# Channel mixing by Strassen's seven products, in two phases

## The chip, the cores and the metric

The kernel runs on one core of one Trainium2 chip. Its engines are TensorE (PE in the profile; PEld are its weight loads), VectorE (DVE), ScalarE (ACT), GpSimd (POOL) and SyncE (SP, which only issues DMAs here). Each has its own queue and takes instructions in order; they wait for each other by semaphores. The metric is the device time of one execution in microseconds (us), the median of several runs.

## The reference

One layer of an encoder trunk on x of 1024 tokens by 1024 channels, float32: a token-mixing part (a gated delta rule beside a spatial gate, joined and projected by w_out, then a layer norm), and a channel-mixing part with a hidden width of 2816, which is all that the change touches:

```python
x = layer_norm(DEEPNORM_ALPHA * x + h @ w_out[l], ln1_g[l], ln1_b[l])
up = causal_depthwise_conv(x @ w_up[l], conv_ffn[l])          # w_up [1024, 5632], 3 taps
a_ff, b_ff = jnp.split(up, 2, axis=-1)
x = layer_norm(DEEPNORM_ALPHA * x + (jax.nn.silu(a_ff) * b_ff) @ w_down[l], ln2_g[l], ln2_b[l])
```

## The kernel before

A wide product keeps float32's accuracy by splitting each operand into a rounded part (hi, a cast on ScalarE) and the remainder (lo, a subtraction on VectorE that reads the operand and hi, both in SBUF), and adding hi·hi, hi·lo and lo·hi. That is `split` (L87 to 89). Every product of 128 x 128 weights with 512 columns is three matmuls.

The channel mixing (L873 on) goes through 22 blocks f of 128 hidden channels. `ffn_up(f)` loads and splits two weight blocks (`load_w`, L349: the a half and the b half), and makes two products of 1024 columns (`proj_half`, L363 to 369), 96 matmuls. The result stays in PSUM; the convolution reads it there, its first tap on ScalarE (L390), two on VectorE (L392). Then silu on ScalarE (L892), the multiplication by b on VectorE (L894), a split of the result into two SBUF slots, and a load and split of a row block of w_down (L903). `ffn_down` multiplies a group of two f (the last group has four) with its w_down rows and adds the result to y in SBUF on VectorE (L925, L927), 48 matmuls for each f. Group g - 1's down product stands behind the first up product of group g, so TensorE always has one while the other's operands are made. No activation of the channel mixing leaves SBUF. In the last group, each row block's layer norm follows its last product (L929 to 958).

The order of the work is set by a scheduler from the program's order and priorities; the W_out product ahead (L835) and its layer norm (`wout_end`) lead into the channel mixing.

Of the kernel before, what the change touches and what calls it, by code (L numbers as in the profile page):

```python
# [996 lines left out]
```

## Time and profile before

| | |
|---|---|
| device time, median of 3 runs | 1558.77 us (1558.72 to 1560.59) |
| span of the profiled execution | 1559.6 us |
| TensorE busy | 1512.3 us, 97% |
| VectorE, ScalarE, GpSimd busy | 54%, 26%, 16% |
| chain that ended last: TensorE's share | 83% |
| HBM read and written | 75.63 MB and 4.19 MB |

The profile is of one execution; its span is the time from the first to the last instruction. A window row gives the busy time of each engine in a stretch, a timeline row one instruction (or several alike) with its start and length, a group row the count, the total and the mean of all instructions of one line and shape, with the idle time of the engine ahead of them.

### The profile page before, as it was taken

What the parts mean: (1) busy time and instruction counts of PE and PEld (TensorE: products, weight loads), DVE (VectorE), ACT (ScalarE), POOL (GpSimd) and SP (SyncE); (2) the same over time, 40 slices, a digit from 0 to 9 for tenths busy, and PEclk for the clock granted to TensorE, in tenths of its full rate; (3) what the DMA queues carried; (4) which work ended last, traced back from release to release, by engine and by line L of the source; (5) the groups of instructions that cost most, each with busy time, mean ns of one, the idle gap of its engine ahead of it and who ended that gap; (6) DMA issues with size and microseconds to landing.
All of it is one profiled execution on the core that took longest, in us unless ns stands there. A gap on an engine that the chain in (4) does not pass through costs nothing.

```text
span 1559.6 us, 17452 instructions
## 1 busy us (share of the span) xinstructions
PE 1512.3 (97%) x7155; PEld 1239.2 (79%) x7155; DVE 841.5 (54%) x1357; ACT 410.7 (26%) x526; POOL 250.2 (16%) x322
## 2 busy tenths in 40 slices
PE   8999899989899999999999999999999999999997
PEld 8977777767778888887888888888888888888885
DVE  5848577785974112335664535455454454635457
ACT  3343333433432111223013211313122131221321
POOL 2344353543531000000210000000000000000007
PEclk9999999999999999999999999999999999999998
DMA  7011101110101111225001211212111020111102
GB/s 233 18 38 41 28 20 36 28 28 28 28 14 41 41 54 55 81 68 201 16 14 60 62 41 41 64 31 68 40 41 55 28 81 28 54 41 41 54 27 108
DMA packets 100798, 80.94 MB, mean 52 GB/s; under 512 B 4155, under 2 KB 90863, under 8 KB 100719
## 3 DMA queue, kind: packets, MB, share of 16 engines
q1 hardware_dynamic: 98991, 73.54, 15.6%
q10 hardware_dynamic: 1728, 6.29, 1.2%
q8 instruction: 56, 0.92, 0.2%
q14 instruction: 23, 0.19, 0.0%
HBM read 75.63 MB, written 4.19 MB: 51 GB/s over the span
## 4 chain that ended last, share of the span: by engine, by line
PE 83%; DVE 10%; DMA 2%; POOL 2%; issue 1%; ACT 1%; SPq 0%; DVEq 0%; POOLq 0%
PE mm L367 49%; PE sm L920 15%; PE mm L437 6%; PE mm L835 4%; PE mm L215 2%; DVE u L582 2%; DVE u L583 1%; DVE y L392 1%; PE sm L613 1%; PE sm L161 1%; PE sm L618 1%; DMA y<-in_x_dram 1%; DVE zz L526 1%; DVE xx L585 1%; DVE dd L524 1%
## 5 line engine op out<-in xcount | busy, mean ns | idle before, releaser
L367 PE MATMUL mm<-xh,wh 128*128 128x512 f32 x2560 | 653.2, 399 | 0.0
L367 PEld LDWEIGHTS mm<-xh,wh 128*128 128x128 f32 x2560 | 477.8, 189 | 101.1 <-issue 0.2
L367 PE MATMUL mm<-xh,wl 128*128 128x512 f32 x1280 | 344.4, 404 | 0.0
L367 PEld LDWEIGHTS mm<-xh,wl 128*128 128x128 f32 x1280 | 240.7, 190 | 54.3
L89 DVE TENSOR_TENSOR wl<-wr,wh 128x1024 fp32r<-128x1024 f32 x63 | 77.2, 1225 | 330.7 <-PE mm L367 285.7
L88 ACT CAST wh<-wr 128x1024 fp32r<-128x1024 f32 x63 | 66.1, 1050 | 486.1 <-PE mm L367 455.6
L221 POOL TENSOR_SCALAR rstd<-mv 128x1 f32<-128x1 f32 x24 | 21.0, 874 | 1043.0 <-DVE mv L817 1019.3
L927 DVE TENSOR_TENSOR y<-y,sm 128x512 f32<-128x512 f32 x144 | 97.2, 684 | 59.4 <-PE sm L920 59.4
L392 DVE SCALAR_TENSOR_TENSOR y<-mm,cf,y 128x1023 f32<-128x1023 f32 x88 | 112.6, 1280 | 16.1 <-ACT y L390 14.9
L920 PE MATMUL sm<-ob,dd 128*128 128x512 f32 x288 | 82.1, 394 | 0.0
L358 POOL TENSOR_TENSOR wl<-wr,wh 128x1024 fp32r<-128x1024 f32 x25 | 60.2, 2408 | 76.2 <-ACT wh L357 23.4
L920 PE MATMUL sm<-ob,kv 128*128 128x512 f32 x240 | 69.1, 395 | 0.0
L920 PE MATMUL sm<-ob,xx 128*128 128x512 f32 x240 | 68.7, 394 | 0.0
L920 PEld LDWEIGHTS sm<-ob,dd 128*128 128x128 f32 x288 | 54.0, 188 | 13.1 <-DVE dd L89 0.2
L390 ACT ACTIVATE y<-mm,cf 128x1024 f32<-128x1024 f32 x44 | 49.2, 1119 | 45.8 <-PE mm L367 45.8
L89 DVE TENSOR_TENSOR ob<-wr,ob 128x1024 fp32r<-128x1024 f32 x26 | 31.8, 1225 | 53.6 <-ACT ob L88 53.6
L920 PE MATMUL sm<-ob,gm 128*128 128x512 f32 x192 | 60.3, 395 | 0.0
L392 DVE SCALAR_TENSOR_TENSOR y<-mm,cq,y 128x1023 f32<-128x1023 f32 (+2 forms) x36 | 45.9, 1276 | 20.5 <-ACT y L390 20.2
L920 PEld LDWEIGHTS sm<-ob,xx 128*128 128x128 f32 x240 | 45.0, 188 | 10.9
L920 PEld LDWEIGHTS sm<-ob,kv 128*128 128x128 f32 x240 | 45.0, 188 | 10.8
L835 PE MATMUL mm<-ob,xh 128*128 128x512 f32 x192 | 47.9, 397 | 0.9 <-DVE y L842 0.9
L835 PEld LDWEIGHTS mm<-ob,xh 128*128 128x128 f32 x192 | 35.8, 188 | 9.6 <-DVE y L842 1.3
(303 smaller groups left out, 1902.9 us busy)
## 6 DMA issues: line engine op xcount, KB each, us to landing
wr<-in_w_up_dram SPq DMA_DIRECT2D x44, 512.0 KB, 3.7
wr<-in_w_in_dram SPq DMA_DIRECT2D x36, 512.0 KB, 3.9
wr<-in_w_down_dram SPq DMA_DIRECT2D x22, 512.0 KB, 3.5
y<-in_x_dram SPq DMA_DIRECT2D x8, 512.0 KB, 6.9
wr<-in_w_out_dram SPq DMA_DIRECT2D x8, 512.0 KB, 3.6
y<-in_x_dram ACTq DMA_DIRECT2D x8, 512.0 KB, 5.7
out_dram<-y SPq DMA_DIRECT2D x16, 256.0 KB, 2.0
ob<-in_w_in_dram SPq DMA_DIRECT2D x8, 256.0 KB, 5.4
```

The costliest lines, as they stand in the source:

```text
L88: nc.scalar.copy(hi, src)
L89: eng.tensor_tensor(out=lo, in0=src, in1=hi.bitcast(F32), op=ALU.subtract)
L215: nc.tensor.matmul(pp[:, 512 * i:512 * i + 260], st, mv[:, 260 * i:260 * i + 260], start=(k, a, b) == (0, 0, 0), stop=(k, a, b) == (KT - 1 ...
L358: nc.gpsimd.tensor_tensor(out=lo, in0=raw, in1=hi.bitcast(F32), op=ALU.subtract)
L367: nc.tensor.matmul(pp[:, half * 512:(half + 1) * 512], w[a][:, k, wcol:wcol + P], act[b][half][:, k], start=n == 0, stop=n == 3 * nk - 1)
L390: nc.scalar.activation(dst, pp, AF.Copy, scale=taps[n - 1])
L392: nc.vector.scalar_tensor_tensor(out=dst[:, s:], in0=pp[:, :S - s], scalar=taps[n - 1 - s], in1=dst[:, s:], op0=ALU.mult, op1=ALU.add)
L437: nc.tensor.matmul(pp[:, half * 512:(half + 1) * 512], w[a][:, k, wcol:wcol + P], o[k][b][:, half], start=n == 0, stop=n == 11)
L582: nc.vector.tensor_tensor(out=tmp[:, :, :i + 1], in0=LB[:, :, :i + 1, i], in1=x16[:, :, :i + 1], op=ALU.mult)
L835: nc.tensor.matmul(pp[:, nh * 512:(nh + 1) * 512], hT[a][half][:, k, off:off + P], wo[k][b][:, nh * 512:(nh + 1) * 512], start=k == 0 and ...
L920: nc.tensor.matmul(pd, f[a][:, m * P:(m + 1) * P], wd[b][:, nh * 512:(nh + 1) * 512], start=n == 0, stop=n == 3 * n_k - 1)
L927: nc.vector.tensor_tensor(out=ys, in0=ys, in1=pd, op=ALU.add)
```

## The change

Both products of the channel mixing go by one level of Strassen's algorithm (in Winograd's form): operands are cut into 2 x 2 blocks, and seven products of sums and differences of blocks take the place of eight.

In the up phase a product's left side is a weight block pair: a11 and a12 are the two halves (512 input channels each) of the a block of f, a21 and a22 those of the b block. Four sums s1 to s4 are formed on GpSimd (`sums`), and seven operands are split (`left_op`). The right sides B1 to B7 are blocks of x1 (the layer norm's output, transposed) and their differences, built once (`x1_first`, `x1_second`). Seven products of 12 matmuls go into PSUM banks X, Z and Y, some of them on top of what the bank holds, after ScalarE has copied it out. In the order of the program the products' left sides are a11, s1, s2, s4, s3, a12, a22: they are called the first to the seventh product. The convolution now reads SBUF. The result of f stays in SBUF until its pair is done; then four sums of the pair are formed on GpSimd, and seven blocks go to HBM (fd0 to fd6). The residual y goes there too (yd).

When all 22 f are done the SBUF places change hands: w_down (`DQ`) and y are loaded, and seven products follow, each over 11 pairs j, with the activations loaded from HBM block by block (`load_f`), split, and multiplied; a product's four banks are added to y at its end. Places of SBUF are reused as soon as what stood there has been read (`reuse_waits="tile"`).

```diff
+    def x1_first(m):
+        cols = slice(m * P, m * P + P)
+        raw = tl("y8", [2, 4, P])
+        for g, pt in enumerate(x1_blocks(m)):
+            half_split(B[(1, 2)[g]], cols, pt)
+            nc.scalar.copy(raw[:, g], pt)
+        first_half.append(raw)
+    def x1_second(m):
+        cols = slice((m - 4) * P, (m - 4) * P + P)
+        raw = first_half[m - 4]
+        p12, p22 = x1_blocks(m)
+        b12t4 = tl("wl", [2, 4, P])
+        t12 = tl("y8", [2, 4, P])
+        t3 = tl("y8", [4, P])
+        b12, t4 = b12t4[:, 0], b12t4[:, 1]
+        t1, t2 = t12[:, 0], t12[:, 1]
+        nc.scalar.copy(b12, p12)
+        nc.vector.tensor_tensor(out=t1, in0=p12, in1=raw[:, 0], op=ALU.subtract)
+        half_split(B[3], cols, p22)
+        nc.vector.tensor_tensor(out=t3, in0=p22, in1=b12, op=ALU.subtract)
+        nc.vector.tensor_tensor(out=t2, in0=p22, in1=t1, op=ALU.subtract)
+        nc.gpsimd.tensor_tensor(out=t4, in0=raw[:, 1], in1=t2, op=ALU.subtract)
+        half_split(B[5], cols, t1)
+        half_split(B[6], cols, t2)
+        half_split(B[7], cols, t3, nc.gpsimd)
+        half_split(B[4], cols, t4, nc.gpsimd)
...
+            B[1], B[2] = new_b(big, "xh", 4), new_b(big, "xh", 4)
             for i in range(4):
-                to_x1(i)
+                x1_first(i)
+    phase["sb"].close()
+    right = enter("right", side="right")
+    B[3], B[5] = new_b(big, "xh", 4), new_b(big, "xh", 4)
+    for i in (6, 7, 4):
+        B[i] = new_b(right, "xh2", 3)
     for m in range(4, NT):
-        to_x1(m)
+        x1_second(m)
...
+    def left_op(src):
+        op = right.tile([P, 2, 512], F32R, tag="op", name=name("op"), bufs=7)
+        split(op[:, 0], op[:, 1], src)
+        return op
+    def block_product(pp, a, b, first=False):
+        n = 0
+        for i, j in TERMS:
+            for k in range(4):
+                nc.tensor.matmul(pp, a[:, i, k * P:(k + 1) * P], b[:, j, k], start=first and n == 0, stop=n == 11,
+                                 skip_group_check=not first)
+                n += 1
+    def sums(s12, s34, a11, a12, a21, a22):
+        s1, s2, s3, s4 = s12[:, 0], s12[:, 1], s34[:, 0], s34[:, 1]
+        for o, a, b, op in ((s1, a21, a22, ALU.add), (s2, s1, a11, ALU.subtract), (s3, a11, a21, ALU.subtract),
+                            (s4, a12, s2, ALU.subtract)):
+            nc.gpsimd.tensor_tensor(out=o, in0=a, in1=b, op=op)
+        return s1, s2, s3, s4
+    def conv3(src, dst, f):
+        nc.scalar.activation(dst, src, AF.Copy, scale=cf[:, 2, f:f + 1])
+        for s in (1, 2):
+            nc.vector.scalar_tensor_tensor(out=dst[:, s:], in0=src[:, :S - s], scalar=cf[:, 2 - s, f:f + 1],
+                                           in1=dst[:, s:], op0=ALU.mult, op1=ALU.add)
+    H0, H1 = slice(0, 512), slice(512, 1024)
     def ffn_up(f):
+        ws = []
+        for c in (f, NF + f):
+            w = left.tile([P, 1024], F32, tag="wq", name=name("wq"), bufs=4)
+            nc.sync.dma_start(v3(w, KT), upsrc[:, :, c * P:(c + 1) * P])
+            ws.append(w)
+        a11, a12, a21, a22 = ws[0][:, H0], ws[0][:, H1], ws[1][:, H0], ws[1][:, H1]
+        s1, s2, s3, s4 = sums(yy([2, 512]), yy([2, 512]), a11, a12, a21, a22)
+        x, z, yb = bank("X", 3), bank("Z", 3), bank("Y", 2)
+        part, mid = yy([2, 512]), yy([512])
+        ca, cb = yy([S]), yy([S])
+        ta, tb = yy([S]), yy([S])
+        block_product(x, left_op(a11), B[1], True)
+        nc.scalar.copy(part[:, 0], x)
+        block_product(z, left_op(s1), B[5], True)
+        nc.scalar.copy(mid, z)
+        block_product(x, left_op(s2), B[6])
+        nc.scalar.copy(part[:, 1], x)
+        block_product(z, left_op(s4), B[3])
+        nc.vector.tensor_tensor(out=ca[:, H1], in0=z, in1=part[:, 1], op=ALU.add)
+        block_product(x, left_op(s3), B[7])
+        nc.vector.tensor_tensor(out=cb[:, H1], in0=x, in1=mid, op=ALU.add)
+        block_product(yb, left_op(a12), B[2], True)
+        nc.vector.tensor_tensor(out=ca[:, H0], in0=yb, in1=part[:, 0], op=ALU.add)
+        conv3(ca, ta, f)
+        nc.scalar.activation(ta, ta, AF.Silu)
+        block_product(x, left_op(a22), B[4])
+        nc.scalar.copy(cb[:, H0], x)
+        conv3(cb, tb, NF + f)
+        nc.vector.tensor_tensor(out=ta, in0=ta, in1=tb, op=ALU.mult)
+        return ta
+    for j in range(NF // 2):
+        f0 = ffn_up(2 * j)
+        nc.sync.dma_start(fd[0][j], f0[:, H0])
+        f1 = ffn_up(2 * j + 1)
+        s = sums(yy([2, 512]), yy([2, 512]), f0[:, H0], f1[:, H0], f0[:, H1], f1[:, H1])
+        for i, src in ((1, f1[:, H0]), (3, f1[:, H1]), (4, s[0]), (5, s[1]), (6, s[2]), (2, s[3])):
+            nc.sync.dma_start(fd[i][j], src)
+    for what in ("left", "ups", "right", "big"):
+        phase[what].close()
...
+    DQ = {}
+    for t in ("b11", "b12", "b22", "b21", "tt"):
+        DQ[t] = dn.tile([P, NJ, 512], F32, tag=t, name=t)
+    for t, two, hs in (("b11", 0, H0), ("b12", 0, H1), ("b22", 1, H1), ("b21", 1, H0)):
+        for c0, c1 in ((0, 2), (2, 4), (4, 7), (7, NJ)):
+            nc.sync.dma_start(DQ[t][:, c0:c1], dnsrc[two][:, c0:c1, hs])
+    y = []
+    for m in range(NT):
+        yt = dn.tile([P, D], F32, tag="y", name=name("y"), bufs=8)
+        nc.scalar.dma_start(yt, yd[m])
+        y.append(yt)
+    lt = dn.tile([P, 2, 1024], F32, tag="lt", name="lt")
+    nc.scalar.dma_start(lt[:, 0], ln2_g[0].partition_broadcast(P))
+    nc.scalar.dma_start(lt[:, 1], ln2_b[0].partition_broadcast(P))
...
+    def load_f(i, j):
+        t = dn.tile([P, 512], F32, tag="fq", name=name("fq"), bufs=6)
+        nc.sync.dma_start(t, fd[i][j])
+        return t
...
+    def down_product(banks, i, right_of, first=False):
+        for j in range(NJ):
+            a = split4(op4(), load_f(i, j))
+            b = split4(op4(), right_of(j))
+            for m in range(4):
+                for n, (p, q) in enumerate(TERMS):
+                    nc.tensor.matmul(banks[m], a[:, p, m * P:(m + 1) * P], b[:, q], start=first and j == 0 and n == 0,
+                                     stop=j == NJ - 1 and n == 2, skip_group_check=not first)
...
+    def t_sum(a, b, dst):
+        def make(j):
+            nc.gpsimd.tensor_tensor(out=DQ[dst][:, j], in0=DQ[a][:, j], in1=DQ[b][:, j], op=ALU.subtract)
+            return DQ[dst][:, j]
+        return make
...
+    X, Z = four("DX"), four("DZ")
+    down_product(X, 0, lambda j: DQ["b11"][:, j], True)
+    to_y(X, 0, H0)
+    down_product(Z, 4, t_sum("b12", "b11", "tt"), True)
+    to_y(Z, 1, H1)
+    down_product(X, 5, t_sum("b22", "tt", "tt"))
+    to_y(X, 0, H1)
+    down_product(Z, 2, lambda j: DQ["b22"][:, j])
+    to_y(Z, 0, H1)
+    down_product(X, 6, t_sum("b22", "b12", "b12"))
+    to_y(X, 1, H1)
+    Y = four("DZ")
+    for j in range(NJ):
+        t_sum("b21", "tt", "tt")(j)
+    down_product(Y, 1, lambda j: DQ["b21"][:, j], True)
+    to_y(Y, 0, H0)
+    for m in range(4):
+        st6 = dn.tile([P, 12], F32, tag="stl", name=name("stl"), bufs=4)
+        for i in range(2):
+            ln_half(y[m], st6, i)
+        finish(m, st6)
...
+        hi, lo, hw = (r[:, j] for r in res)
+        if j % 2 == 0:
+            pair = op4()
+        lw = pair[:, j % 2]
+        split(hi, lo, load_f(3, j))
+        split(hw, lw, DQ["tt"][:, j])
+        last.append(((hi, lo), (hw, lw)))
+    st = {m: dn.tile([P, 12], F32, tag="stl", name=name("stl"), bufs=4) for m in range(4, NT)}
+    for m in range(4, NT):
+        ln_half(y[m], st[m], 1)
+    for m in range(4):
+        for j in range(NJ):
+            for n, (p, q) in enumerate(TERMS):
+                nc.tensor.matmul(X[m], last[j][0][p][:, m * P:(m + 1) * P], last[j][1][q], start=False,
+                                 stop=j == NJ - 1 and n == 2, skip_group_check=True)
+        one_to_y(X[m], 4 + m, H0)
+        ln_half(y[4 + m], st[4 + m], 0)
+        finish(4 + m, st[4 + m])
```

The first place is GpSimd's queue. Before, there is nothing on it between the last rows of the first layer norm and the last layer norm at the kernel's end (mv and rstd are their statistics):

```order
L222 TENSOR_TENSOR rstd_872_6150<-rstd_872_6150,nhalf_107 128x1
L221 TENSOR_SCALAR rstd_876_6211<-mv2_875_6209 128x1
L222 TENSOR_TENSOR rstd_876_6211<-rstd_876_6211,nhalf_107 128x1
L221 TENSOR_SCALAR rstd_1366_10325<-mv2_1365_10323 128x1
L222 TENSOR_TENSOR rstd_1366_10325<-rstd_1366_10325,nhalf_107 128x1
L952 TENSOR_TENSOR mv2_1365_10323<-mv2_1365_10323,rstd_1366_10325 128x1
```

Now, at the pair of f = 2 and 3 and the next even f = 4 (yy_959 and yy_979 are the results of f = 2 and 3, yy_988 and yy_989 the pair's sums; wq_990 and wq_991 are the weights of f = 4, yy_992 and yy_993 their sums s1 to s4, wq_1010 and wq_1011 those of f = 5):

```order
L975 TENSOR_TENSOR yy_988_6955<-yy_959_6693,yy_979_6833 128x512
L975 TENSOR_TENSOR yy_989_6956<-yy_959_6693 128x512
L975 TENSOR_TENSOR yy_988_6955<-yy_988_6955,yy_959_6693 128x512
L975 TENSOR_TENSOR yy_992_6971<-wq_991_6969 128x512
L975 TENSOR_TENSOR yy_989_6956<-yy_979_6833,yy_988_6955 128x512
L975 TENSOR_TENSOR yy_992_6971<-yy_992_6971,wq_990_6967 128x512
L975 TENSOR_TENSOR yy_993_6972<-wq_990_6967,wq_991_6969 128x512
L975 TENSOR_TENSOR yy_993_6972<-wq_990_6967,yy_992_6971 128x512
L975 TENSOR_TENSOR yy_1012_7111<-wq_1011_7109 128x512
L975 TENSOR_TENSOR yy_1013_7112<-wq_1010_7107,wq_1011_7109 128x512
```

The weight sums of f = 4 stand behind three of the pair's sums, which need the finished yy_979.

The second place is ScalarE's queue. Before, while TensorE is at one f (y8_1048 and y8_1049 are the two halves of an f's convolution, wh and ob casts of weights, xx of an activation):

```order
L88 CAST wh_1056_7700<-wr_1055_7699 128x1024
L390 ACTIVATE y8_1048_7679<-mm_1046_7581,cf_101_893 128x1024
L892 ACTIVATE y8_1048_7679<-y8_1048_7679 128x1024
L88 CAST ob_1068_7824<-wr_1067_7823 128x1024
L88 CAST wh_1059_7706<-wr_1058_7705 128x1024
L390 ACTIVATE y8_1049_7680<-mm_1047_7582,cf_101_893 128x1024
L88 CAST xx_1050_7689<-y8_1048_7679 128x1024
```

Now, from the silu of f = 3 on (op_1004 to op_1009 are the operands of f = 4 from its second product on, op_1023 the first of f = 5; Z_995 and X_994 are banks of f = 4):

```order
L1011 ACTIVATE yy_979_6833<-yy_979_6833 128x1024
L111 CAST op_1004_7002<-yy_992_6971 128x512
L999 COPY yy_997_6980<-X_994_6977 128x512
L111 CAST op_1005_7018<-yy_992_6971 128x512
L111 CAST op_1006_7034<-yy_993_6972 128x512
L111 CAST op_1007_7050<-yy_993_6972 128x512
L111 CAST op_1008_7066<-wq_990_6967 128x512
L111 CAST op_1009_7086<-wq_991_6969 128x512
L111 CAST op_1023_7126<-wq_1010_7107 128x512
L1001 COPY yy_998_6981<-Z_995_6978 128x512
L1003 COPY yy_997_6980<-X_994_6977 128x512
```

The copy of bank Z, which holds the second product of f = 4, stands behind the casts of all of that f's operands and of the next f's first.

The third place is SP's queue where the phases meet. Before, the weights of up and down products come in turn:

```order
L355 DMA wr_1086_7957<-in_w_up_dram 128x8x128
L355 DMA wr_1089_7963<-in_w_up_dram 128x8x128
L903 DMA wr_1098_8081<-in_w_down_dram 128x1024
L355 DMA wr_1101_8087<-in_w_up_dram 128x8x128
L355 DMA wr_1104_8093<-in_w_up_dram 128x8x128
```

Now, from the last pair's blocks on (yy_9452 is the result of f = 21 and yy_9574, yy_9575 are the last pair's sums; b_9596 to b_9599 are the four quarters of w_down, fq an activation block of the first down product):

```order
L1024 DMA fd_5687<-yy_9574 128x512
L1024 DMA fd_5688<-yy_9574 128x512
L1024 DMA fd_5689<-yy_9575 128x512
L1024 DMA fd_5685<-yy_9575 128x512
L1039 DMA b_9596<-in_w_down_dram 128x2x512 x2
L1039 DMA b_9596<-in_w_down_dram 128x3x512
L1039 DMA b_9596<-in_w_down_dram 128x4x512
```

and, at the end of these loads:

```order
L1039 DMA b_9598<-in_w_down_dram 128x4x512
L1039 DMA b_9599<-in_w_down_dram 128x2x512 x2
L1039 DMA b_9599<-in_w_down_dram 128x3x512
L1039 DMA b_9599<-in_w_down_dram 128x4x512
L1051 DMA fq_9645<-fd_5683 128x512
L1051 DMA fq_9665<-fd_5683 128x512
```

The first activation block stands behind all sixteen loads of w_down, and these behind the last pair's stores.

## Rows read from the trace of the kernel before

**Rows 1.** The page: the span, part 1 (engines), the chain that ended last by engine.

```profile
span 1559.6 us, 17452 instructions
PE 1512.3 (97%) x7155; PEld 1239.2 (79%) x7155; DVE 841.5 (54%) x1357; ACT 410.7 (26%) x526; POOL 250.2 (16%) x322
PE 83%; DVE 10%; DMA 2%; POOL 2%; issue 1%; ACT 1%; SPq 0%; DVEq 0%; POOLq 0%
```

**Rows 2.** Windows: us, busy (x records) by engine, TensorE clock, DMA share, GB/s.

```profile
core 0: us, PE busy (x) PEld busy (x) DVE busy (x) ACT busy (x) POOL busy (x), PEclk, DMA share, GB/s
811.50:1548.40 736.90, 736.90 (x3201) 597.83 (x3199) 370.81 (x398) 173.96 (x167) 27.97 (x42) 1.00 0.16 49
900.00:1000.00 100.00, 100.00 (x434) 81.20 (x433) 45.93 (x47) 22.16 (x21) 0.00 (x0) 1.00 0.16 48
```

**Rows 3.** Timeline of TensorE where the channel mixing begins: start, duration, line.

```profile
810.75 0.85 PE L835 MATMUL mm<-xx,xh 128*128 128x512 f32 x3
811.44 1.91 PE L161 MATMUL sm<-ident,y 128*128 128x128 f32 x16
```

**Rows 4.** Groups by line and shape: engine, tiles, count; busy us, mean ns; idle before.

```profile
L88 ACT CAST xh<-y 128x512 fp32r<-128x512 f32 x16 | 8.8, 617 | 15.4 <-DVE y L794 9.5 <-PE mm L367 5.9
L89 DVE TENSOR_TENSOR xh<-y,xh 128x512 fp32r<-128x512 f32 x16 | 10.0, 685 | 5.3 <-PE mm L367 4.0 <-ACT xh L88 1.4
L88 ACT CAST xh<-sm 128x512 fp32r<-128x512 f32 x32 | 17.4, 592 | 68.2 <-PE sm L161 67.7
L390 ACT ACTIVATE y<-mm,cf 128x1024 f32<-128x1024 f32 x44 | 49.2, 1119 | 45.8 <-PE mm L367 45.8
L392 DVE SCALAR_TENSOR_TENSOR y<-mm,cf,y 128x1023 f32<-128x1023 f32 x44 | 56.3, 1280 | 14.9 <-ACT y L390 14.9
L894 DVE TENSOR_TENSOR y<-y,y 128x1024 f32<-128x1024 f32 x22 | 26.9, 1222 | 0.5
L933 POOL TENSOR_TENSOR y<-y,xh 128x512 f32<-128x512 f32 x14 | 17.8, 1291 | 1.2 <-DVE y L930 1.2
L927 DVE TENSOR_TENSOR y<-y,sm 128x512 f32<-128x512 f32 x144 | 97.2, 684 | 59.4 <-PE sm L920 59.4
```

**Rows 5.** Timeline of VectorE and GpSimd working beside each other, from 185.8 us.

```profile
185.83 1.05 POOL L481 TENSOR_TENSOR gm<-triM,gt 128x512 fp32r<-128x512 f32 x1 [1.81 <-PE sm L486]
185.92 2.04 DVE L424 TENSOR_TENSOR y<-y,ob 128x1024 f32<-128x1024 f32 x1
190.09 1.26 POOL L490 TENSOR_TENSOR dd<-dd,triS 128x512 f32<-128x512 f32 x1
190.15 1.74 DVE L685 TENSOR_TENSOR kv<-kv,rstd 128x512 f32<-128x512 f32 x1 [2.19 <-POOL rstd L222]
191.42 1.60 POOL L491 TENSOR_TENSOR dd<-dd,triM 128x512 f32<-128x512 f32 x1
```

**Rows 6.** Windows where TensorE restarts after idling (columns as in rows 2).

```profile
332.50:335.00 2.50, 0.49 (x2) 0.53 (x3) 1.82 (x4) 0.00 (x0) 1.58 (x2) 0.58 0.00 0
335.00:337.50 2.50, 2.50 (x9) 1.92 (x9) 0.57 (x2) 1.16 (x2) 0.68 (x1) 0.50 0.00 0
337.50:340.00 2.50, 2.50 (x14) 2.40 (x13) 1.94 (x11) 0.12 (x2) 0.00 (x0) 0.56 0.00 0
340.00:342.50 2.50, 2.50 (x15) 2.06 (x14) 1.82 (x2) 1.85 (x3) 1.49 (x1) 1.00 0.00 0
```

**Rows 7.** The same view of the first input loads, the densest DMA of the span.

```profile
12.00:15.00 3.00, 3.00 (x27) 3.00 (x26) 2.06 (x3) 0.74 (x2) 0.00 (x0) 1.00 1.03 412
```

**Rows 8.** The page, part 6: DMA issues, KB each, us from issue to landing.

```profile
wr<-in_w_up_dram SPq DMA_DIRECT2D x44, 512.0 KB, 3.7
```

**Rows 9.** Timeline of the span's end, from TensorE's last matmuls.

```profile
1547.59 0.86 PE L920 MATMUL sm<-ob,dd 128*128 128x512 f32 x3
1548.33 2.23 DVE L930 TENSOR_TENSOR y<-y,xh 128x1024 f32<-128x1024 f32 x1 [1.22 <-ACT y L954]
1550.48 0.67 DVE L927 TENSOR_TENSOR y<-y,sm 128x512 f32<-128x512 f32 x1
```

More of the change, by code (lines that the diff above doesn't have):

```diff
@@ L46, in trunk, with enter @@
     nc = tc.nc
-    sb = ctx.enter_context(tc.tile_pool(name="sb", bufs=1))
-    ps = ctx.enter_context(tc.tile_pool(name="ps", bufs=1, space=bass.MemoryType.PSUM))
+    keep = ctx.enter_context(tc.tile_pool(name="keep", bufs=1))
+    dr = ctx.enter_context(tc.tile_pool(name="dr", bufs=1, space=bass.MemoryType.DRAM))
+    phase = {}
+    def enter(what, **kw):
+        s = ExitStack()
+        phase[what] = s
+        return s.enter_context(tc.tile_pool(name=what, bufs=1, reuse_waits="tile", **kw))
+    big = enter("big")
+    sb = enter("sb", side="right")
+    act = enter("act")
+    ps = enter("ps", space=bass.MemoryType.PSUM)
+    KEEP = {"rstd", "mv2", "st6", "cf"}
+    POOL_OF = {"xh": big, "y8": act, "wr": act, "wh": act, "wl": act}
     count = [0]
@@ L800, in trunk @@
         load_wo((SLOTS[2 * k], SLOTS[2 * k + 1]))
-    lnp = [tl("y8", [D]) for _ in range(2)]
+    lnp = [tl("wh", [D]) for _ in range(2)]
     nc.scalar.dma_start(lnp[0], ln1_g[0].partition_broadcast(P))
@@ new lines, in trunk, with yy, bank @@
+    for m in range(4, NT):
+        x1_second(m)
+    phase["act"].close()
+    phase["ps"].close()
+    left = enter("left")
+    ps = enter("ups", space=bass.MemoryType.PSUM)
+    upsrc = w_up[0].rearrange("(k p) c -> p k c", p=P)
+    def yy(shape, dt=F32):
+        return left.tile([P] + shape, dt, tag="yy", name=name("yy"), bufs=11)
+    def bank(tag, bufs):
+        return ps.tile([P, 512], F32, tag=tag, name=name(tag), bufs=bufs)
+    def left_op(src):
+        op = right.tile([P, 2, 512], F32R, tag="op", name=name("op"), bufs=7)
+        split(op[:, 0], op[:, 1], src)
+        return op
@@ new lines, in trunk @@
+    ps = ctx.enter_context(tc.tile_pool(name="dps", bufs=1, space=bass.MemoryType.PSUM, reuse_waits="tile"))
+    NJ = NF // 2
+    dnsrc = w_down[0].rearrange("(j two p) c -> two p j c", two=2, p=P)
+    outv = out[0].rearrange("(t p) d -> t p d", p=P)
+    DQ = {}
[4 more added lines that the diff above has]
+            nc.sync.dma_start(DQ[t][:, c0:c1], dnsrc[two][:, c0:c1, hs])
@@ new lines, in four, with to_y, one_to_y @@
+    def four(tag):
+        return [ps.tile([P, 512], F32, tag=tag, name=name(tag), bufs=4) for _ in range(4)]
+    seen = set()
+    def to_y(banks, row, hs):
+        for m in range(4):
+            one_to_y(banks[m], 4 * row + m, hs)
+    def one_to_y(bank_, m, hs):
+        ys = y[m][:, hs]
+        if (m, hs.start) in seen:
+            nc.vector.tensor_tensor(out=ys, in0=ys, in1=bank_, op=ALU.add)
+        else:
+            seen.add((m, hs.start))
+            nc.vector.scalar_tensor_tensor(out=ys, in0=ys, scalar=ALPHA, in1=bank_, op0=ALU.mult, op1=ALU.add)
@@ new lines, in trunk @@
+    to_y(Y, 0, H0)
+    for m in range(4):
+        st6 = dn.tile([P, 12], F32, tag="stl", name=name("stl"), bufs=4)
+        for i in range(2):
+            ln_half(y[m], st6, i)
+        finish(m, st6)
+    last = []
+    res = [dn.tile([P, NJ, 512], F32R, tag=t, name=f"{t}r") for t in ("b11", "b12", "b22")]
+    for j in range(NJ):
[6 more added lines that the diff above has]
+        last.append(((hi, lo), (hw, lw)))
```

141 lines of the change are left out of this document (43 added, 98 removed).

## Prediction

> **What bounds the kernel now.** I read the page first: TensorE is busy for 97% of the 1559.6 us, and the chain that ended last runs through it for 83% [rows 1]. The windows say where: from the end of the W_out product to the last matmul of the kernel TensorE never idles, 736.9 of 736.9 us at full clock, and in a clean stretch it does 434 matmuls of 512 columns per 100 us, so 0.2304 us each [rows 2]. VectorE is half busy there, ScalarE a fifth, GpSimd not at all. The timeline puts the beginning of the stretch at 811.5 us [rows 3] and its end at 1548.4, with 11.2 us of last layer norm behind it [rows 9]. So matmuls taken away here come off the time in full, unless TensorE begins to wait. The rest of the argument is about waits, for which I take the durations of the operand work [rows 4], of VectorE beside GpSimd [rows 5], of the clock after idling [rows 6] and of dense DMA [rows 7, 8].
>
> **What goes.** Before: 22 x 96 matmuls up and 22 x 48 down, 3168. After: 7 products of 12 for each f, 22 x 84 = 1848, and 7 x 11 x 12 = 924 down, 2772. 396 x 0.2304 = 91.2 us go. 3168 x 0.2304 = 729.9 of the 736.9 us; the other 7.0 (transposes, mostly) stay. TensorE's own work after is 2772 x 0.2304 + 7.0 = 645.7 us. All up to 811.5 keeps its order.
>
> **What comes: the stall on each even f.** GpSimd now forms four weight sums for each f, and four sums of the finished activations for each pair; its queue has the pair's sums ahead of the next even f's weight sums (the first place shown with the change). The pair's sums wait for the product silu(a)·b of the odd f, which needs that f's seventh product. Call T the end of that product. ScalarE copies it (0.59), makes the first tap (1.12), VectorE two taps (2 x 1.28) and the multiplication (1.22): T + 5.5 [rows 4]. GpSimd's 512-column sum took 1.29, 1.26 and 1.05 in three places [rows 4, 5]; I take 1.25. Three of the pair's four sums: T + 9.3; the first weight sum of the even f: T + 10.5; its cast 0.62: T + 11.2. Meanwhile TensorE has only the first product of that f (12 x 0.2304 = 2.77, its operand is a raw block). So it idles from T + 2.8 to T + 11.2, 8.4 us.
>
> Then the fourth product. Its operand, the last of GpSimd's next four sums, would be ready at 15.5, and with two of VectorE's remainders (0.69 each) taking turns with them at T + 17. But the fourth product adds to bank Z, which still holds the second until ScalarE has copied it, and that copy stands on ScalarE behind the casts of s4, s3, a12, a22 and of the next f's a11 (the second place): 17 + 5 x 0.62 + 0.59 = T + 20.7. The last four products take 11.1: T + 31.8, where 7 x 2.77 = 19.4 would do. That is 12.4 us lost for each of f = 2, 4, ... 20: 10 x 12.45 = 125 us. The lower end is the first wait alone, 8.4 x 10 = 84; the upper end has 2 us more per stall (below), 145.
>
> The odd f have no such wait: their weight sums stand right behind and need only weights, which land 3.7 us after issue [rows 8], loaded an f ahead. Per f VectorE has 7 remainders x 0.685, 4 taps x 1.28, 1.22 and 3 additions from PSUM x 0.684, 13.2 us; 11.1 of them read two SBUF operands. GpSimd has 6 sums x 1.25 = 7.5. Each fits in 19.4. They do not run beside each other, though: a two-operand VectorE instruction of 1.22 took 2.04 when GpSimd was 0.1 us ahead of it, one of 0.69 took 1.74, and GpSimd's next took 1.60 [rows 5]. 11.1 + 7.5 = 18.6 of 19.4 still fits, with no room to spare. **The Trainium skill** (GPSIMD Engine Reference, Specifications) says that GpSimd shares its SBUF interfaces with VectorE and contends with VectorE instructions that have two SBUF inputs; this trace agrees (2.04 for 1.22). By that rule the odd f may lose time too; this is a rival below.
>
> The clock: behind a pause TensorE ran at 0.50 to 0.58 of its full clock (the 1.2 GHz level) through two windows of steady work, and at full clock in the next [rows 6]; about 4 us of matmuls at half clock cost 2 us. In the stall this falls on the second and third products, which then end at about T + 19, still ahead of the copy at T + 20.7, so it costs nothing in my sum. **The Trainium skill** (TensorE: Matmul & The Clock Gate, HAM oscillation) warns that a kernel which leaves TensorE idle between bursts pays again and again to get its clock back. If the fourth product were slow as well, 2 us would come on top at each of the ten stalls, 20 us: 1682 for the forecast's 1662.
>
> **The seam before the up products.** Five of the seven right-hand blocks are combinations of both halves of x1, and their tiles come free only when the last W_out matmul (811.5) has read its operands. Behind it VectorE finishes the last row block's layer norm and makes 24 pieces of 0.69 (about 21 us), with GpSimd's 12 of 1.25 taking turns for part of it (3 to 6 us more). The load of f = 0's second weight block waits for a place that one of those pieces reads, so it starts 21 to 26 us after the last matmul; 3.7 to land, 1.25 for the sum, 0.62 for the cast: the second product starts near 811.5 + 29.5. The first product (2.8) and transposes (3.8, in the 7.0) lie within it: 23 us lost. 3.4 more because the copy of f = 0's first product stands behind five casts, and 2 for the clock: 28, bounds 20 and 33.
>
> **The seam between the phases.** The down phase reads what the up phase stored, and the whole of w_down (5.77 MB) stands on SP's queue ahead of the first activation block; y (4.2 MB) and the norm's tables (1 MB) come on ScalarE's queue at the same time. SP's queue is held by the last pair's stores until the fourth sum, T + 5.5 + 4 x 1.25 = T + 10.5 (the third place). The densest stretch of the trace moved 412 GB/s [rows 7]: 11 MB are 26.7 us, 5.77 MB alone 14. The first block lands between T + 25 and T + 38; y's loads begin at most a few us before SP's, so I take T + 36.5. With the first cast and remainder (1.3) and the clock (2): 40 us lost, bounds 30 and 50.
>
> **The down phase and the end.** For each j of a product (2.77) VectorE has 1.37 and GpSimd 1.25, in all 2.62: it fits. The last product's 44 casts and remainders are done beside the sixth (22 x 0.69 on VectorE, 30.4 us there). I put 3 us for the change-overs between products. The last addition stood behind a 2.23 us instruction (1548.33) before [rows 9]; it doesn't now: the tail is 9.2 rather than 11.2.
>
> **Sum.** 811.5 + 645.7 + 125 + 28 + 40 + 3 + 9.2 = 1662.4, against the profiled 1559.6. That execution is 0.8 us above the median of 1558.77, so 1661 in device time: 6.6% slower, a gain of 91 buried under 196 of waits. Bounds of the four terms together: 1600 to 1700.
>
> **The rivals.**
> 1. *Slower, but less*: the copy of the second product isn't late (the casts find their sums early), so each pair loses only 8.4 us. Ten times 4 less: 1621. For it: GpSimd's spans are rough, its shortest sum took 1.05 [rows 5]; against it: in-order ScalarE.
> 2. *Taking turns binds every f*: with GpSimd's sums at the 1.60 seen in contention [rows 5], an odd f needs 13.2 + 6 x 1.6 = 22.8 instead of 19.4; 3.4 x 12 periods is 41 more: 1702.
> 3. *Faster*: the pair's sums don't hold the weight sums. The place is GpSimd's queue at an even f; the point is whether the first weight sum is ready before T + 2.2, when the first product ends less a cast. Then 125 us fall away: 1536. Against it: the pair's first sum cannot start before T + 5.5 by four durations of [rows 4], and the queue is in order.
> 4. *The plain gain*: all seams hidden as well, 1559.6 - 91 - 2 = 1466. Against it: the seam between the phases is a true dependence of 10.5 us, and the bytes.
>
> **How the numbers follow.** Forecast 0.66 (1635 to 1690 on its own), rival 1 0.13, rival 2 0.07, rival 3 0.10, rival 4 0.02; the last 0.02 lies about no change. Faster 0.12, within 0.2% (about what a measurement of this kernel can't tell from no change) 0.02, slower 0.86. The range 1600 to 1702 takes in the forecast and rivals 1 and 2, with 0.14 left out.
>
> **What would show it.** Right: TensorE about 83% busy from 811 on; a gap of 8 us after the first product of each even f and a shorter one after its third, the releaser GpSimd's sum through a ScalarE cast, then ScalarE's copy; periods of 19.4 and 31.8 us in turn; one gap near 23 us at the beginning and one near 38 in the middle, with DMA at 400 GB/s. Wrong: equal periods near 19.4 (rival 3) or 22 (rival 2), or matmuls of the up phase at half clock throughout.

## The result

The changed kernel takes 1682.59 us (median of 4 runs, 1676.78 to 1683.57) against 1558.85: 1.078 times the time before (95% interval 1.076 to 1.080). Forecast was 1661, 1600 to 1702. The profiled execution's span is 1681.6 us. HBM reads rose from 75.63 to 100.01 MB and writes from 4.19 to 28.57 MB: the activations and y, stored and loaded again.

The page, the lines that answer to [rows 1]: TensorE's share of the span fell from 97% to 86%, its share of the chain from 83% to 47%; 23% is "issue" now, time in which nothing that the profile shows was waited for.

```profile
span 1681.6 us, 17855 instructions
PE 1440.4 (86%) x6759; PEld 1184.8 (70%) x6759; DVE 968.2 (58%) x1527; ACT 549.1 (33%) x858; POOL 510.6 (30%) x510
PE 47%; issue 23%; DVE 12%; POOL 12%; DMA 4%; ACT 2%; SPq 1%; POOLq 0%; DVEq 0%
```

The windows of the stages, as [rows 2] (columns: from:to, length, busy time and records of PE, PEld, DVE, ACT and POOL, TensorE's clock, DMA share, GB/s). They are, in turn: the seam from the last W_out matmul to the end of f = 0; the up products of f = 1 to 21; the seam between the phases; the first down product; down products two to seven; the end.

```profile
812.20:868.40 56.20, 28.85 (x117) 22.54 (x116) 39.68 (x43) 20.43 (x36) 31.19 (x22) 0.73 0.23 66
868.40:1389.50 521.10, 427.00 (x1765) 344.56 (x1763) 309.74 (x315) 193.74 (x294) 170.26 (x120) 0.91 0.24 75
1389.50:1447.40 57.90, 0.05 (x1) 0.00 (x0) 6.14 (x6) 3.95 (x6) 30.04 (x25) 0.53 0.92 339
1447.40:1482.20 34.80, 32.57 (x132) 26.45 (x133) 21.26 (x32) 15.56 (x28) 5.71 (x5) 0.90 0.41 116
1482.20:1661.80 179.60, 179.60 (x793) 148.54 (x792) 121.71 (x175) 75.92 (x129) 47.20 (x49) 1.00 0.33 96
1661.80:1681.60 19.80, 0.12 (x1) 0.00 (x0) 8.84 (x11) 2.48 (x2) 9.40 (x15) 0.61 0.29 106
```

In 868.4 to 1389.5 TensorE is busy for 427 of 521 us, at a mean clock of 0.91; for 58 us between the phases it does nothing; and for 20 us after its last matmul the kernel is not done, where before it was 11.2 [rows 9]. Only down products two to seven run as the whole stretch did before [rows 2]: 179.6 of 179.6.

One period of the up phase, from the timeline (start, duration, engine, line, what; in brackets the idle time before and what ended it). The first row is the seventh product of an odd f and the first of the next even f; the odd f ends at T = 1038.4.

```profile
1035.72 5.60 PE L967 MATMUL X<-xh,op 128*128 128x512 f32 x24
1038.64 0.59 ACT L1013 COPY yy<-X 128x512 f32<-128x512 f32 x1 [0.84 <-PE X L967]
...
1043.15 1.22 DVE L1015 TENSOR_TENSOR yy<-yy,yy 128x1024 f32<-128x1024 f32 x1
1044.45 1.26 POOL L975 TENSOR_TENSOR yy<-yy,yy 128x512 f32<-128x512 f32 x1 [33.01 <-DVE yy L1015]
...
1046.89 1.26 POOL L975 TENSOR_TENSOR yy<-yy,yy 128x512 f32<-128x512 f32 x1
1048.11 1.26 POOL L975 TENSOR_TENSOR yy<-wq 128x512 f32<-128x512 f32 x1
...
1049.40 0.62 ACT L111 CAST op<-yy 128x512 fp32r<-128x512 f32 x1 [7.88 <-POOL yy L975]
...
1050.07 1.22 PE L967 MATMUL Z<-xh,op 128*128 128x512 f32 x2 [8.75 <-ACT op L111]
```

Copy (1038.64), taps, multiplication (1043.15), three of the pair's sums (the row left out between the two shown is one of them), the first weight sum (1048.11), its cast (1049.40), and only then the second product, after 8.75 us of idling. The weight sum begins as the third of the pair's sums ends, so what it waited for last was its turn. The same place 50.1 us earlier shows the fourth product's wait: 0.75 us, for ScalarE's copy L1001 of bank Z behind the casts; the second product before it took 4.93 us rather than 2.9, at a granted clock of 0.50 (the 1.2 GHz level) from 999.9 to 1002.4.

```profile
999.95 4.93 PE L967 MATMUL Z<-xh,op 128*128 128x512 f32 x12 [8.76 <-ACT op L111]
...
1004.72 2.89 PE L967 MATMUL X<-xh,op 128*128 128x512 f32 x12
...
1006.17 1.66 ACT L111 CAST op<-wq 128x512 fp32r<-128x512 f32 x3
...
1007.73 0.57 ACT L1001 COPY yy<-Z 128x512 f32<-128x512 f32 x1
...
1008.36 3.02 PE L967 MATMUL Z<-xh,op 128*128 128x512 f32 x12 [0.75 <-ACT yy L1001]
```

The seam between the phases: SyncE's queue holds w_down's loads until 1433.8, and the first cast of an activation block comes at 1446.2, 56.7 us after the last up product (1389.5). The stores hold SyncE's queue until 1400.9. From there to 1433.8 the DMA engines are busy throughout, at 377 GB/s.

```profile
1391.42 23.48 ACTq L1043 DMA_DIRECT2D y<-yd  x8
...
1395.35 5.44 SPq L1024 DMA_DIRECT2D fd<-yy  x6
...
1400.88 32.84 SPq L1039 DMA_DIRECT2D b<-in_w_down_dram  x16
...
1433.76 31.33 SPq L1051 DMA_DIRECT2D fq<-fd  x15
...
1446.24 0.62 ACT L111 CAST dop<-fq 128x512 fp32r<-128x512 f32 x1 [53.77 <-DMA fq<-fd]
...
1447.43 0.79 PE L1068 MATMUL DX<-dop,dop 128*128 128x512 f32 x1 [57.88 <-ACT dop L111]
```

The end: the last matmul begins at 1661.5, but the last two additions of banks to y (L1086) each stand behind the multiplication L1095 of an earlier row block's layer norm, which waits for ScalarE.

```profile
1661.53 0.39 PE L1149 MATMUL DX<-b22r,b12r 128*128 128x512 f32 x1
...
1665.09 1.23 DVE L1095 TENSOR_TENSOR y<-y,lt 128x1024 f32<-128x1024 f32 x1 [4.50 <-ACT y L1106]
1666.23 0.68 DVE L1086 SCALAR_TENSOR_TENSOR y<-y,DX 128x512 f32<-128x512 f32 x1
...
1671.69 1.23 DVE L1095 TENSOR_TENSOR y<-y,lt 128x1024 f32<-128x1024 f32 x1 [3.74 <-ACT y L1106]
1672.83 0.68 DVE L1086 SCALAR_TENSOR_TENSOR y<-y,DX 128x512 f32<-128x512 f32 x1
```

And the beginning of the up phase: f = 0's weights are asked for only at 828.2, its first cast comes at 841.1, behind the blocks of x1, and the first product follows 14.1 us after the last transposes.

```profile
828.18 29.79 SPq L990 DMA_DIRECT2D wq<-in_w_up_dram  x6
...
841.10 0.61 ACT L111 CAST op<-wq 128x512 fp32r<-128x512 f32 x1
...
841.76 5.46 PE L967 MATMUL X<-xh,op 128*128 128x512 f32 x12 [14.11 <-ACT op L111]
...
853.04 4.63 PE L967 MATMUL X<-xh,op 128*128 128x512 f32 x12 [3.08 <-ACT yy L999]
```

### The profile page after: what moved, and what is told of

Its sections match the earlier page's. It is cut to its first block, busy times and chain, and to the rows that moved or that the text cites. A ratio compares the mean times of both kernels' runs of the same rounds, so it can differ in the third digit from the quotient of the medians.

```text
span 1681.6 us, 17855 instructions
## 1 busy us (share of the span) xinstructions
PE 1440.4 (86%) x6759; PEld 1184.8 (70%) x6759; DVE 968.2 (58%) x1527; ACT 549.1 (33%) x858; POOL 510.6 (30%) x510
## 3 DMA queue, kind: packets, MB, share of 16 engines
HBM read 100.01 MB, written 28.57 MB: 76 GB/s over the span
## 4 chain that ended last, share of the span: by engine, by line
PE 47%; issue 23%; DVE 12%; POOL 12%; DMA 4%; ACT 2%; SPq 1%; POOLq 0%; DVEq 0%
PE mm L390 17%; POOL yy L975 8%; PE DX L1068 5%; PE mm L858 5%; PE mm L460 5%; PE DZ L1068 5%; PE mm L238 2%; DVE u L605 2%; DVE u L606 1%; DVE y L415 1%; PE X L967 1%; DMA b<-in_w_down_dram 1%; POOL y L1098 1%; DMA fq<-fd 1%; DVE op L112 1%
## 5 line engine op out<-in xcount | busy, mean ns | idle before, releaser
L390 PE MATMUL mm<-xh,wh 128*128 128x512 f32 x1152 | 313.9, 407 | 0.0
L967 PE MATMUL X<-xh,op 128*128 128x512 f32 x1056 | 255.3, 395 | 17.4 <-ACT op L111 14.4
L967 PEld LDWEIGHTS X<-xh,op 128*128 128x128 f32 x1056 | 201.7, 191 | 61.2 <-ACT op L111 15.2
L390 PEld LDWEIGHTS mm<-xh,wh 128*128 128x128 f32 x1152 | 213.4, 190 | 40.6 <-issue 0.4
L967 PE MATMUL Z<-xh,op 128*128 128x512 f32 x528 | 150.0, 440 | 93.8 <-ACT op L111 87.6
L967 PEld LDWEIGHTS Z<-xh,op 128*128 128x128 f32 x528 | 112.0, 216 | 127.1 <-ACT op L111 92.0
L390 PE MATMUL mm<-xh,wl 128*128 128x512 f32 x576 | 160.5, 405 | 0.0
L1068 PE MATMUL DX<-dop,dop 128*128 128x512 f32 x396 | 92.9, 397 | 60.1 <-ACT dop L111 57.9
L112 DVE TENSOR_TENSOR op<-yy,op 128x512 fp32r<-128x512 f32 x88 | 84.7, 983 | 98.9 <-ACT op L111 98.7
L981 DVE SCALAR_TENSOR_TENSOR yy<-yy,cf,yy 128x1023 f32<-128x1023 f32 x88 | 112.4, 1283 | 28.7 <-ACT yy L979 27.4
L390 PEld LDWEIGHTS mm<-xh,wl 128*128 128x128 f32 x576 | 106.9, 190 | 20.3
L112 DVE TENSOR_TENSOR dop<-fq,dop 128x512 fp32r<-128x512 f32 x66 | 53.1, 804 | 109.3 <-ACT dop L111 109.3
L112 DVE TENSOR_TENSOR wl<-wr,wh 128x1024 fp32r<-128x1024 f32 x19 | 23.2, 1223 | 97.0 <-PE mm L390 71.4
```

Source lines behind the costliest of these rows:

```text
L112: eng.tensor_tensor(out=lo, in0=src, in1=hi.bitcast(F32), op=ALU.subtract)
L390: nc.tensor.matmul(pp[:, half * 512:(half + 1) * 512], w[a][:, k, wcol:wcol + P], act[b][half][:, k], start=n == 0, stop=n == 3 * nk - 1)
L967: nc.tensor.matmul(pp, a[:, i, k * P:(k + 1) * P], b[:, j, k], start=first and n == 0, stop=n == 11, skip_group_check=not first)
L981: nc.vector.scalar_tensor_tensor(out=dst[:, s:], in0=src[:, :S - s], scalar=cf[:, 2 - s, f:f + 1], in1=dst[:, s:], op0=ALU.mult, op1=ALU.add)
L1068: nc.tensor.matmul(banks[m], a[:, p, m * P:(m + 1) * P], b[:, q], start=first and j == 0 and n == 0, stop=j == NJ - 1 and n == 2, skip_gro ...
```

## The experiments

Each is a variant of the changed kernel, whose 1682.6 us are the measure; ratios are to the kernel before. Beside these runs the kernel before took 1561.5 to 1562.5 us and not 1558.9, so a difference from 1682.6 is uncertain by some 3 us. The code shown is cut.

**The pair's sums one f later on GpSimd's queue** (e_later).

```diff
+            f1 = ffn_up(2 * j + 1, weights(2 * j + 1))
+            if j < NF // 2 - 1:
+                w = weights(2 * j + 2)
+            s = sums(one("pair", [2, 512], 2), one("pair", [2, 512], 2), f0[:, H0], f1[:, H0], f0[:, H1], f1[:, H1])
```

`weights` holds the loads and the four weight sums of an f. The edit also gives sums, copies and results SBUF tiles of their own, which were drawn from one common set before, and writes GpSimd's order out.

> Up phase only: each even f's weight sums are put ahead of the previous pair's sums on GpSimd's queue (with tiles of their own for the sums), nothing else. Theory (the queue order makes the stall): the profile of the changed kernel shows a period of 50.07 us for a pair of f where 28 x 0.2267 x 6 = 38.1 us of matmuls stand in it; the 12.0 us per pair go, 10 x 12.0 = 120 us, so 1682.6 - 120 = about 1563 us, and equal periods near 19.1 us for each f. Rival (VectorE and GpSimd taking turns bind): GpSimd's sums of 1.26 to 1.74 us beside VectorE's 11.1 us of two-operand work make 18.7 to 21.5 us for each f, so periods up to 21.5 and a time up to 1615 us. Rival (the wait was not the queue's but the weights' arrival or the convolution's): 1670 to 1685 us.

1621.4 us (ratio to before 1.038, 1.037 to 1.040). 61 of the 120 us went. The wait for the cast is gone, and another stands in its place, ten times 4.0 us (waits of TensorE by line: total, times, longest; then the timeline):

```profile
PE X L967 <- DVE cb L1014: 39.8, 10, 4.0
```

```profile
1035.58 1.72 POOL L975 TENSOR_TENSOR ws<-wq,ws 128x512 f32<-128x512 f32 x1
...
1037.32 1.14 ACT L111 CAST op<-ws 128x512 fp32r<-128x512 f32 x2 [2.75 <-POOL ws L975]
1037.97 1.09 DVE L112 TENSOR_TENSOR op<-ws,op 128x512 fp32r<-128x512 f32 x1 [1.21 <-ACT op L111]
...
1038.99 0.68 DVE L1014 TENSOR_TENSOR cb<-X,mid 128x512 f32<-128x512 f32 x1
...
1039.72 1.59 PE L967 MATMUL X<-xh,op 128*128 128x512 f32 x5 [4.02 <-DVE cb L1014]
```

VectorE's addition L1014, which frees bank X for the seventh product, stands behind the remainder of an operand of the next f (L112, 1037.97), whose weight sum GpSimd finished at 1037.3, because the pair's sums now stood ahead of the odd f's weight sums. The theory named the right queue but looked one step only. Of the two rivals neither holds: 1621 lies above the one's range and below the other's, and what is left is one wait in each pair.

**The pair's sums on VectorE** (e_vec): `nc.vector` for `nc.gpsimd` in the four sums of a pair.

> Up phase only: the four sums of each pair are made on VectorE instead of GpSimd; the order of everything else is left to the scheduler. Theory (the even f waits because its weight sums stand behind the pair's sums): GpSimd no longer waits for the product silu(a)b, so the casts of the even f's operands come early, but VectorE now has the four sums (4 x 0.69) ahead of the remainders of that f, which the last four matmuls of its second product need: they wait until about 9 us after the odd f's end instead of 4.6, so 4.4 us of the 12.0 remain per pair: 1682.6 - 76 = about 1606 us. Rival (GpSimd's place doesn't matter, the dependence on the product silu(a)b does, by VectorE's own order): 8 to 12 us per pair remain: 1645 to 1682 us.

1624.1 us (1.040, 1.038 to 1.041), 58 less and not 76. As expected the second product starts early and stops before its last four matmuls, which need a remainder that stands behind the four sums; the pause is 3.0 us, with 1.3 before the product and the clock's fall behind it. This edit left the tiles as they were.

```profile
PE Z L967 <- DVE op L112: 30.1, 10, 3.0
...
PE Z L967 <- ACT op L111: 13.0, 11, 1.3
```

**The pair's sums behind both following weight sums** (e_later2).

```diff
+            f0 = ffn_up(2 * j, w0)
+            nc.sync.dma_start(fd[0][j], f0[:, H0])
+            w1 = weights(2 * j + 1)
+            if pair is not None:
+                pair_out(j - 1, *pair, nc.sync)
+            f1 = ffn_up(2 * j + 1, w1)
```

`pair_out` makes the sums and stores of the pair before.

> Up phase only: on GpSimd's queue each pair's sums now stand behind the weight sums of both f that follow the pair (one f later than in e_later), so that no weight sum waits for the product silu(a)b. In e_later 4.0 us per pair were left before the seventh product of the even f, ended by VectorE's addition L1014, which stood behind the remainder of an operand of the next f whose weight sum was behind the pair's sums; with the clock's fall after it 5.8 us per pair. Theory (all of the stall is the queues' order): no wait longer than 0.5 us in the up phase, pairs of 38.1 us, 1621.4 - 58 = about 1563 us. Rival (VectorE and GpSimd taking turns bind once the order is right): pairs of 40 to 43 us, 1585 to 1615 us.

1562.1 us (1.0003, 0.999 to 1.001): the whole stall is gone. In 400 us of the up phase TensorE is busy for 399.9, at full clock:

```profile
866.00:1266.00 400.00, 399.93 (x1765) 330.88 (x1763) 306.27 (x310) 194.88 (x289) 176.44 (x116) 1.00 0.30 97
```

So the order on GpSimd's queue made the stall, 120 us of it. Order and tiles of their own were not tried apart; that the order is the cause is read from the changed kernel's row 1048.11 and from e_vec. That VectorE and GpSimd take turns doesn't bind the up phase: it shows in the durations (groups by line and shape of e_later2: count, busy, mean ns), 1111 ns for the remainder of a weight sum where one takes 685 alone [rows 4] and up to 1716 ns for a sum, and 19.04 us still hold them.

```profile
L112 DVE TENSOR_TENSOR op<-ws,op 128x512 fp32r<-128x512 f32 x88 | 97.7, 1111 | 34.4 <-ACT op L111 33.9
...
L975 POOL TENSOR_TENSOR ws<-wq,ws 128x512 f32<-128x512 f32 x22 | 37.8, 1716 | 0.0
```

**The loads of the second phase in the order of their use** (e_loads): the first quarter of w_down and the activation blocks in turn, then one further load behind each activation block, all on SyncE's queue.

```diff
+    load_dq("b11", 0)
...
+            raw = load_f(i, j)
+            if j < len(later.get(i, ())):
+                what, *args = later[i][j]
+                what(*args)
```

`later` lists the other quarters, y and the tables.

> Between the phases only: the first quarter of w_down and the activation blocks of the first down product are loaded ahead, the other quarters, y and the norm's tables in the order of their use beside the first three products; all on SyncE's queue. Theory (the restart waits for bytes that stand ahead of the first activation block): in the changed kernel the first product began 57.9 us after the up phase's end, with 18.4 MB moved at 390 GB/s; now 1.3 MB stand ahead, so it begins near 16 us after the up phase's end, held by the last pair's stores until 11.4: 40 us less, about 1642 us, unless loads are late later in the first product (a few us). Rival (the wait is the drain of the up phase, casts and clock, not the bytes): under 15 us less, 1668 us or more.

1646.1 us (1.054, 1.052 to 1.055), 36.5 less. TensorE's wait fell from 57.9 to 17.0 us. Some 5 came back: the second product had 35.5 us instead of 29.9, because GpSimd's sums of w_down, which ran during the wait before, now run beside the product. A remainder of VectorE that comes behind the start of such a sum takes 1.78 us, VectorE is busy for all 35.6 us of the product, and where two such remainders stand in a step it takes 3.4 us and not 2.72, with a wait of 0.4 us:

```profile
PE DX L1083 <- ACT dop L111: 17.0, 1, 17.0
```

```profile
1436.97 1.07 PE L1083 MATMUL DZ<-dop,dop 128*128 128x512 f32 x4
...
1459.62 3.04 PE L1083 MATMUL DZ<-dop,dop 128*128 128x512 f32 x12 [0.38 <-DVE dop L112]
1463.02 3.04 PE L1083 MATMUL DZ<-dop,dop 128*128 128x512 f32 x12 [0.36 <-DVE dop L112]
...
1472.48 0.39 PE L1083 MATMUL DX<-dop,dop 128*128 128x512 f32 x1
```

**VectorE's order in the last product** (e_tail): the additions of finished banks first, the multiplications L1095 of row blocks 4 to 6 behind them.

> The end only: VectorE's order in the last down product is written out so that no addition of a finished bank stands behind the multiplication of an earlier row block's layer norm, which waits for ScalarE. Theory: in the changed kernel the last matmul ends near 1661.8 us and the last addition begins at 1672.8, since each row block's norm passes through VectorE, GpSimd, ScalarE and VectorE again in 6.6 us with the next addition behind it; now the last addition begins within 1 us of the last matmul and the last norm ends 8 to 10 us earlier: about 1673 us. Rival (the norms themselves are the bound, GpSimd's additions and stores of the last row blocks): 1678 to 1683 us.

1677.3 us (1.073, 1.071 to 1.075), 5 less, between theory and rival: the last addition now begins 0.4 us after the last matmul does, but GpSimd's four additions of two earlier row blocks (6.4 us) now run beside VectorE's last two instructions, which took 3.42 us instead of 1.42. How much of the rest of the end that explains wasn't tried.

**All three** (e_best): e_later2, e_loads and e_tail together.

> e_later2 with the loads of e_loads and the end of e_tail. Theory (the three costs are in different stretches and add): 1682.6 - 119 - 36.5 - 5.3 = about 1522 us, 2.5% faster than the kernel before. Rival (what one edit gives another takes back, by DMA in the first down product or by the clock): 1535 us or more.

1522.2 us, 0.975 of before (0.973 to 0.977). The costs add within 2 us (120.5, 36.5 and 5.3 against 160.4).

**The last pair's stores on GpSimd's queue** (e_bestP).

> e_best with the six stores of the last pair issued by GpSimd, which makes its sums, instead of SyncE. In e_loads SyncE's queue was held by these stores until 11.4 us after the up phase's end and the first down product began 17.0 us after TensorE's last matmul. Theory (that queue is the rest of the wait): the first quarter's loads start at the up phase's end, the first product about 8 to 10 us earlier: about 1513 us. Rival (the rest of the wait is the transfers and casts themselves): within 3 us of e_best.

1511.9 us, 0.968 (0.966 to 0.970): 10.3 less than e_best, as the theory had it. Of the 17.0 us wait of e_loads 4.1 are left, and 3.3 for a remainder behind it:

```profile
PE DX L1101 <- ACT dop L111: 4.1, 1, 4.1
```

**Where the up phase begins** (e_seam, e_seam2, e_seam3).

> e_bestP with two changes where the up phase begins: f = 0's weights are loaded into a place that is free earlier (the places of the up phase are laid out so that they don't stand on the blocks still in use), and the remainders of B7 go from GpSimd to VectorE. In the changed kernel the weights' load began 16 us after the last W_out matmul, TensorE's first product 29.5 us after it, and its seventh ended after 56 us with 23.5 us of work in them. Theory (late weights and GpSimd's 12 blocks set this seam): 6 to 12 us less than e_bestP, about 1504 us. Rival (the 24 blocks on VectorE set it, which has more to do now): the same as e_bestP or up to 3 us more.

1511.9 us (0.968, 0.966 to 0.970): nothing gained. Counted from the transposes behind the last W_out matmul the first product began 2.3 us earlier than in e_bestP, but the second waited 2.6 us for the sum's cast, and second and third began at the same 34.5 and 41.3 us. The sum itself was held by a load:

```profile
838.72 1.26 POOL L975 TENSOR_TENSOR ws<-wq 128x512 f32<-128x512 f32 x1 [4.16 <-DMA wq<-in_w_up_dram]
```

GpSimd's last block ended at 834.6, and only then was f = 0's second weight block asked for. So the time that the rival gave doesn't show the rival: this edit left the load late.

> e_bestP with f = 0's two weight blocks loaded into two of the operand places, which are free when the last W_out matmul has run, and the cast of its first operand ahead of the casts of the second half's blocks on ScalarE; the weight sums stay behind GpSimd's 12 blocks. In e_bestP TensorE waited 14.1 us for that cast, its first product began 30 us after the last W_out matmul and the third waited 3.7 us more for ScalarE's copy. Theory (the first product and its copy stand behind the blocks only by ScalarE's order and the late load): the first product runs among the transposes, the second begins 2 to 3 us earlier, the third without its wait: 5 to 7 us less than e_bestP's 1511.9, about 1506 us. Rival (GpSimd's blocks and then f = 0's sums set this seam): within 3 us of e_bestP.

1506.9 us, 0.965 (0.964 to 0.967), 5.0 less than e_bestP, as the theory had it. The first product runs among the transposes, and the second waits 14.8 us, for the cast of the first weight sum:

```profile
823.27 4.54 PE L977 MATMUL X<-xh,op 128*128 128x512 f32 x12
...
840.67 1.26 POOL L985 TENSOR_TENSOR ws<-op 128x512 f32<-128x512 f32 x1
...
842.64 5.05 PE L977 MATMUL Z<-xh,op 128*128 128x512 f32 x12 [14.83 <-ACT op L111]
```

> e_seam2 with the remainders of B7 on VectorE instead of GpSimd (8 blocks on GpSimd instead of 12, 28 on VectorE instead of 24). If GpSimd's blocks set when f = 0's sums begin, four blocks of 1.25 to 1.7 us less make 5 us less than e_seam2; if VectorE's blocks set it, up to 3 us more.

1505.3 us, 0.964 (0.962 to 0.966): 1.6 less than e_seam2 with intervals that overlap, so the times don't show whether GpSimd's or VectorE's blocks set this seam. The traces say more:

```profile
837.97 1.70 POOL L985 TENSOR_TENSOR ws<-op 128x512 f32<-128x512 f32 x1
...
840.38 5.49 PE L977 MATMUL Z<-xh,op 128*128 128x512 f32 x12 [10.95 <-ACT op L111]
```

In both the first weight sum begins as GpSimd's last block ends (840.7 and 838.0). Counted from the transposes (810.6 and 811.1) that is 30.1 us in e_seam2 and 26.9 in e_seam3, and the second product comes 2.7 us earlier. So GpSimd's blocks hold the sum, by these two profiled executions. GpSimd's blocks themselves stand behind casts of ScalarE and results of VectorE; what sets their pace stays open. From the last W_out matmul (811.2) to the end of the seventh product (860.2) e_seam3 takes 49.0 us, 25.6 more than the 19.0 of products and 4.4 of transposes in it.

## Why the prediction was right, and where its terms were off

The direction and the mechanism held; 1661 against 1682.6. The signs came as listed: periods of 31.1 and 19.1 us in turn, the long wait behind the first product and the short one behind the third. Term by term, by the windows above:

- **TensorE's work**: 645.7 forecast. In e_later2's window 1765 records fill 400 us, 0.2266 us each, where the kernel before needed 0.2304 [rows 2]; 2772 x 0.2266 and 4.4 of transposes (at full clock) are 632.5. 13 less than forecast. Why a matmul costs 1.6% less here wasn't tried.
- **The stall on each even f**: 125 forecast. 521.1 us for 21 f of 19.04 leave 121; per pair 50.07 - 38.08 = 12.0 for 12.45. The path held: the first wait was 8.75 for 8.4, and the copy of bank Z, which lets the fourth product begin, ended at T + 20.0 for 20.7 (1008.3, where T is 988.3). The fourth product waited only 0.75 us for it, because the second had lost 2 us to the clock before; as the prediction said, that loss lies within the time until the copy. e_later2 shows the whole by taking it away: 120.
- **The seam before the up products**: 28 forecast, 56.2 - 19.0 - 4.4 = 32.8 measured. The step missed that the first product itself waits, 14.1 us, for a cast that stands behind the blocks on ScalarE, and so runs at the lower clock (5.46 us).
- **The seam between the phases**: 40 forecast, bounds 30 and 50; 1482.2 - 1389.5 - 29.9 = 62.8 measured. This is the step that failed, in its size. "The whole of w_down (5.77 MB)" was wrong: 2816 x 1024 floats are 11.5 MB, and with y, the tables and the stores some 18 MB had to move: the window shows 339 GB/s for 57.9 us, 19.6 MB, and not 11 MB in 26.7 us. The hold by the stores was sized rightly: until 1400.9, T + 11.4 for 10.5. The mechanism (bytes ahead of the first activation block, behind stores that wait for GpSimd) is what e_loads and e_bestP took away: 36.5 and 10.3 us.
- **Change-overs of the down products**: 3 forecast, none measured. But that VectorE's 1.37 and GpSimd's 1.25 "fit" in 2.77 held for the second product only because GpSimd's sums ran during the wait; in e_loads it took 35.5 us.
- **The end**: 9.2 forecast, 19.8 measured. The prediction saw that the 2.23 us instruction of [rows 9] was gone, and not that on VectorE's queue the last additions stand behind multiplications that wait for ScalarE; 6.6 us for each row block (1665.09, 1671.69).

The differences, -13.2 - 3.8 + 4.8 + 22.8 - 3.0 + 10.6 and 0.7 for a later W_out end, make 18.9 of the 19.2 us by which the span passed 1662.4. That the time came so near is in part luck: three terms were 20.0 us too large together and three 38.2 too small.

Of the rivals, "slower, but less" does not hold: a pair lost 12.0 us and not 8.4, and the copy was late, though little of its lateness shows as a wait. "Taking turns binds every f" is excluded by e_later2, and the fall of the clock at the fourth product, which would have added 20 us, did not come (3.02 us, the row 1008.36). **The Trainium skill**, GPSIMD Engine Reference (Specifications), has GpSimd contend with VectorE's instructions with two SBUF inputs. This case agrees in the durations (1111 ns for 685 in e_later2), where it doesn't bind, and in e_loads' second product, where it does. That TensorE would be 83% busy from 811 on was a slip: 645.7 of the forecast 841.7 up to the last matmul are 77%; 668.1 of 849.6, 79%, were measured, with the matmuls at the lower clock in them.

## What to carry to other kernels

Fewer matmuls are worth what they take only where the operand work beside them has an order that lets it run ahead: here 91 us of matmuls went and 217 us of waits came in the up phase and its two seams, and changes of order, queue and SBUF places, with the same arithmetic, took 171 us off again (e_bestP). When sums of results and sums of weights share an in-order queue, put those that only need loads ahead of those that need the last result, by as many steps as the queues behind them look ahead: one step left 4.0 us of waiting in each pair here, two left none. Count the bytes that stand ahead of the first block that a phase needs from the tensor's shape.
